# A hybrid decoder layer on one core: three edits at the boundaries of its stages

## Chip, core and metric

The kernel runs on one core of a Trainium2 chip. The metric is the device time of one execution in microseconds (us); less is better. Engines are called by their short names: PE is TensorE, DVE is VectorE, ACT is ScalarE, POOL is GpSimd, SP is SyncE.

## What is computed

One decoder layer over 2048 tokens of width 1024, all in float32. Cut to what matters here:

```python
h = rms_norm(x, pre_mix_norm)
proj = h @ w_in
y_lru = rms_norm(rg_lru(conv(proj_x)) * gelu(proj_gate), lru_out_norm)
y_ssd = rms_norm(ssd_chunked(conv(proj_xbc), dt, ...) * silu(proj_z), ssd_out_norm)
mix = concat(y_lru, y_ssd) @ w_out
x = x + rms_norm(mix, post_mix_norm)
h = rms_norm(x, pre_ffn_norm)
f = (silu(h @ w_gate) * (h @ w_up)) @ w_down
out = x + rms_norm(f, post_ffn_norm)
```

`rms_norm(x, w)` is `x * rsqrt(mean(x * x) + 1e-6) * w` over the 1024 channels of a token. The feed-forward width is 2816.

## The kernel before

**Numbers and products.** Every float32 operand of a large product is split into a rounded part and the rest (`split`, L129 to L134: a cast on ACT, a subtraction on DVE), and a product is three matmuls of 128 x 512 (`mm3`, L136 to L139). Tokens come in two blocks of 1024 (`b`), each of two halves of 512 (`j` or `hh`); a token tile has 128 tokens. The three feed-forward products are done by a seven-product scheme of 2 x 2 blocks (the operands B11, B21, T1 to T4, B22), so that sums and differences of token halves are formed first and kept in DRAM (`h_dr`, `f_dr`, `t_dr`).

**Mixer (to about 1020 us).** For each block, the columns of `w_in` stream through PE in an order written by hand; each product fills a PSUM tile named `pp`. The smaller matmuls (transposes, scans, sums) use PSUM tiles named `pq`. Both names have two buffers. Work on a finished column (`ssd_mix`, `lru_mix`) is a generator, cut by `yield`; the function `site` (L326) advances it, and calls of `site(0)` to `site(3)` stand between the products, `SITES` (L33) saying how many steps each makes. Block 0's last generator ends with `sumsq(b, 0, acc)` (L407): sixteen one-column matmuls of L118 (`rms_of`) against a vector of ones, a copy L120 and the reciprocal root `rstd_of` (L85 to L96: six small DVE operations and a root on ACT). They run at the start of block 1, behind its product for C, and the accumulator that they read is last written by L322. The result is first used in the output projection. Then come, in the program, the convolution of C, `ssd_dt3` (L443 to L459, which reads what L436 writes), `ssd_group2` (transposes L482, scores L488) and the next product.

**Output projection (about 1021 to 1363 us).** For each of 16 token tiles, in the order of `tiles` (L222), two half products go to `pp` and `pq`; L806 and L807 scale and add them; L811 to L815 do the first norm, add the input and write the row to DRAM as `x1_dr`; L816 to L818 do the second norm. The closure `turned` (L758) transposes the normed tile on PE (L761) one tile later and writes its parts to `h_dr`. The last two tiles (fourth token tile of each half of block 1) are not turned: L821 writes them normed to `hl_dr`.

**Gate and up stage (about 1363 to 2210 us).** All PSUM is eight buffers named `pf`. For each block and each of 22 steps `fi`, seven products of 12 matmuls follow each other, each into its own `pf` tile. The tiles for results are named `fo` (12 buffers, function `res`, L909): `f0`, `f1` (written by L935, L941) and, each second step, four sums (L952 to L955). Ahead of the products of steps 3 and 4 of block 0 stands `late_rows` (L855): it loads a tile from `hl_dr`, transposes it (L862), copies it to `fo` (L864) and, with the second, forms the sums L871 to L874 for `h_dr`.

**Down stage (about 2210 us to the end).** The last product, `prod_tiles(1)`, gives one token tile at a time. For each, L1089 adds it into `m1`, `square_mul` squares the row with its sum (L1025) and multiplies it in place with the norm's weight (L1026), `rstd_of` follows, and two L1048 scale it and add `x1`, each followed by a write to the output.

**What sets the order.** A scheduler orders each engine's queue when the kernel is built. Its priority is the order of the program; an instruction that is not ready by its own estimate of times is passed by a later one that is. A tile has a name, and the tiles of one name share that name's buffers.

```python
def site(n):
    if stages:
        for _ in range(SITES[n]):
            if next(stages[0], 1):
                stages.pop()
                break
```

Of the kernel before, what the change touches and what calls it, by code (L numbers as in the profile page):

```python
# [8 lines left out]
F32 = mybir.dt.float32  # L9
F32R = mybir.dt.float32r  # L10
AF = mybir.ActivationFunctionType
ALU = mybir.AluOpType
# [3 lines left out]
P = 128  # L16
T = 2048
D = 1024
KD = D // P
TB = 1024  # L20
NB = T // TB
HB = 512
# [24 lines left out]
def hybrid_layer(ctx: ExitStack, tc: tile.TileContext, x, xT, w_in, w_dt, pack, heads, rows, wa, wx, w_out, w_gu, w_dn, out):  # L47
# [13 lines left out]
    acc_dr = dram.tile([P, TB], F32, name="acc_dr")  # L61
    cs_dr = dram.tile([NB, NH, TB], F32, name="cs_dr")
    h_dr = [[dram.tile([P, 4, HB], F32, name=f"h_dr{b}_{o}") for o in range(7)] for b in range(NB)]
    hl_dr = dram.tile([2, P, D], F32, name="hl_dr")
    f_dr = [[dram.tile([P, KF, HB], F32, name=f"f_dr{b}_{o}") for o in range(7)] for b in range(NB)]
    t_dr = [dram.tile([P, KF, HB], F32, name=f"t_dr{o}") for o in range(4)]

# [2 lines left out]
    def par(n, i=0, w=None):  # L70
        o, full = PK[n]
        return pk[:, o + i:o + i + (w or 1)]
# [188 lines left out]
    with ExitStack() as fr:  # L261
# [112 lines left out]
        def lru_mix(b, i, lx, gl, acc, bdl):  # L374
            th = []
            lh, ll = (tl.tile([P, TB], F32R, name="t4", bufs=NT4) for _ in range(2))
            a.copy(out=lh, in_=lx)
            v.tensor_sub(out=ll, in0=lx, in1=lh.bitcast(F32))
            yield
            for j in range(2):  # L380
                pr = pq.tile([P, TB], F32, name="pq")
                for hh in range(2):
                    s = slice(hh * HB, (hh + 1) * HB)
                    mm3(pr[:, s], bd[:, i, j, :], bdl[i // 4][:, i % 4, j, :], lh[:, s], ll[:, s], True, True)
                t = t4()
                a.activation(out=t, in_=pr, func=AF.Tanh, scale=0.5, bias=hb[:, 8 * j + i:8 * j + i + 1])
                th.append(t)
            ci = c2[:, i:i + 1]
            av = t4()
            a.activation(out=av, in_=th[0], func=AF.Exp, scale=ci, bias=ci)  # L390
            a.activation(out=th[0], in_=th[0], func=AF.Tanh, scale=ci, bias=ci)
            a2 = t4()
            a.activation(out=a2, in_=av, func=AF.Square)
            v.scalar_tensor_tensor(out=a2, in0=a2, scalar=1.0, in1=th[0], op0=ALU.add, op1=ALU.mult)
            v.tensor_scalar(out=a2, in0=a2, scalar1=0.0, scalar2=None, op0=ALU.min)
            a.activation(out=a2, in_=a2, func=AF.Sqrt, scale=-0.25)
            v.scalar_tensor_tensor(out=th[1], in0=th[1], scalar=1.0, in1=lx, op0=ALU.add, op1=ALU.mult)
            v.tensor_mul(out=th[1], in0=th[1], in1=a2)
            v.tensor_tensor_scan(out=th[1], data0=av, data1=th[1], initial=hc[:, i:i + 1], op0=ALU.mult, op1=ALU.add)  # L399
            v.tensor_copy(out=hc[:, i:i + 1], in_=th[1][:, TB - 1:TB])  # L400
            v.tensor_mul(out=gl, in0=th[1], in1=gl)
            spill(gl, i, b)
            accum(gl, th[0], acc, i == 0)
            if i == 7:
                if b + 1 < NB:
                    yield
                    sumsq(b, 0, acc)  # L407
                else:
                    a.dma_start(out=acc_dr, in_=acc)
# [337 lines left out]
    with ExitStack() as orr:  # L747
# [36 lines left out]
        for n, t in enumerate(tiles):  # L784
            gs = gq.pop(0)
            if n == len(tiles) - 2:
                def hook(k):
                    if k % 2 == 0:
                        ops0[k // 2] = build_op(0, k // 2, hx_tile, staged)
                firsts[n] = half(gs, 0)  # L790
                firsts[n + 1] = half(gq[0], 0, hook)
                pre = load_gu(forder[0], lambda: oc.tile([P, 4, HB], F32, name="S"),
                              lambda: splp.tile([P, D], F32R, name="s_hi"), lambda: splp.tile([P, D], F32R, name="s_lo"))
            pss = [firsts.pop(n) if n in firsts else half(gs, 0), half(gs, 1)]
            if turn:
                turn.pop()()
            if n == 4:
                acc = raw_tile()
                sy.dma_start(out=acc, in_=acc_dr)
                sumsq(NB - 1, 0, acc)  # L800
            if n + 2 < len(tiles):
                gq.append(load_g(tiles[n + 2]))
            xnt = oc.tile([P, D], F32, name="xn", bufs=2)
            sy.dma_start(out=xnt, in_=x[t * P:(t + 1) * P, :])
            mx = oc.tile([P, D], F32, name="mx", bufs=2)
            a.activation(out=mx, in_=pss[0], func=AF.Copy, scale=r12[:, 0, t:t + 1])  # L806
            v.scalar_tensor_tensor(out=mx, in0=pss[1], scalar=r12[:, 1, t:t + 1], in1=mx, op0=ALU.mult, op1=ALU.add)  # L807
            junk = oc.tile([P, D], F32, name="ob")
            ss = small.tile([P, 2], F32, name="o_ss")
            rs = small.tile([P, 2], F32, name="o_rs")  # L810
            a.activation(out=junk, in_=mx, func=AF.Square, accum_out=ss[:, 0:1])  # L811
            rstd_of(ss[:, 0:1], rs[:, 0:1], 1)
            v.scalar_tensor_tensor(out=mx, in0=mx, scalar=rs[:, 0:1], in1=pmw, op0=ALU.mult, op1=ALU.mult)
            v.tensor_add(out=mx, in0=mx, in1=xnt)
            a.dma_start(out=x1_dr[t * P:(t + 1) * P, :], in_=mx)  # L815
            a.activation(out=junk, in_=mx, func=AF.Square, accum_out=ss[:, 1:2])  # L816
            rstd_of(ss[:, 1:2], rs[:, 1:2], 1)
            v.scalar_tensor_tensor(out=xnt, in0=mx, scalar=rs[:, 1:2], in1=gpf, op0=ALU.mult, op1=ALU.mult)  # L818
            b, i, j = t // NC, t % 4, (t % NC) // 4
            if b + 1 == NB and i == 3:  # L820
                a.dma_start(out=hl_dr[j], in_=xnt)  # L821
            else:
                turn.append(lambda b=b, i=i, j=j, xnt=xnt: turned(b, i, j, xnt))
    mp.close()

# [6 lines left out]
    with ExitStack() as fa:  # L832
# [21 lines left out]

        def late_rows(j, res):  # L855
            r = raw_tile()
            sy.dma_start(out=r, in_=hl_dr[j])
            xs = []
            for q in range(2):
                ps = bank()  # L860
                for k in range(4):
                    te.transpose(ps[:, k * P:(k + 1) * P], r[:, q * HB + k * P:q * HB + (k + 1) * P], ident)  # L862
                xs.append(res())
                a.copy(out=xs[-1], in_=ps)  # L864
            put = [(B11, xs[0]), (B21, xs[1])] if j == 0 else [(B22, xs[1])]
            if j == 0:
                half0.extend(xs)
            else:
                (x0, x2), (x1, x3) = half0, xs
                t1, t2, t3, t4_ = (res() for _ in range(4))  # L870
                v.tensor_sub(out=t1, in0=x1, in1=x0)  # L871
                v.tensor_sub(out=t2, in0=x3, in1=t1)
                v.tensor_sub(out=t3, in0=x3, in1=x1)
                v.tensor_sub(out=t4_, in0=x2, in1=t2)  # L874
                put += [(T1, t1), (T2, t2), (T3, t3), (T4, t4_)]
            for o, z in put:
                a.dma_start(out=h_dr[NB - 1][o][:, :, 3 * P:], in_=z.rearrange("p (k c) -> p k c", c=P))

        for b in range(NB):
# [6 lines left out]
            for fi, f in enumerate(forders[b]):  # L886
# [22 lines left out]
                def res():  # L909
                    return fo.tile([P, HB], F32, name="fo", bufs=12)  # L910
# [31 lines left out]
                k = f % KF  # L942
# [18 lines left out]
    with ExitStack() as fb:  # L961
# [57 lines left out]
                    mm3(ps, *cur[k], *(z[:, c] for z in bs[k // 2]), k == 0, k == KF - 1)  # L1019
                yield ps  # L1020

        def square_mul(y, t, e):
            junk = fy.tile([P, HB], F32, name="fjunk", bufs=1)
            ss = fy.tile([P, 1], F32, name="f_ss", bufs=4)
            a.activation(out=junk, in_=y[:, t], func=AF.Square, accum_out=ss)  # L1025
            v.tensor_mul(out=y[:, t], in0=y[:, t], in1=pfw[:, e * HB:(e + 1) * HB])  # L1026
            return ss

        def first_half(y, t, e):
# [10 lines left out]
            sy.dma_start(out=xt, in_=x1_dr[rows_of(j, t), :])  # L1040
            return xt

        def second_half(ys, t, j, e, m, xt):
            rs = fy.tile([P, 1], F32, name="f_rs", bufs=2)
            rstd_of(square_mul(ys[e], t, e), rs, 1, m)
            for z, q in ((0, a), (1, sy)):
                h = slice(z * HB, (z + 1) * HB)
                v.scalar_tensor_tensor(out=xt[:, h], in0=ys[z][:, t], scalar=rs, in1=xt[:, h],  # L1048
                                       op0=ALU.mult, op1=ALU.add)
                q.dma_start(out=out[rows_of(j, t), h], in_=xt[:, h])  # L1050

# [33 lines left out]
        for t, p in enumerate(prod_tiles(1)):  # L1085
            ms += [first_half(u2, i, 1) for i in range(len(ms), min(t + 2, NT))]
            if t + 2 < NT:
                xq.append(load_x1(0, t + 2))
            v.tensor_add(out=m1[:, t], in0=p, in1=m1[:, t])  # L1089
            second_half((m1, u2), t, 0, 0, ms[t], xq[t])  # L1090


def _cols(w, n):
# [43 lines left out]
```

## Time and profile before

| | us |
|---|---|
| median of 3 runs | 2634.25 |
| lowest, highest | 2632.26, 2636.03 |
| the profiled execution, its own time | 2635.64 |
| its span, first to last instruction | 2633.8 |
| PE busy in the span | 2613.7 (99%) |
| DVE busy | 1852.7 (70%) |
| ACT busy | 1123.6 (43%) |
| POOL busy | 1.1 (0%) |

Times in the rows below are microseconds from the span's start. A busy engine is one with an instruction in work; matmuls are pipelined, so that one of 0.39 us is followed by the next after 0.227 us. In waits, the engine named behind the arrow is the one that released the waiting one by the profile.

### The profile page before, as it was taken

The page shows a single profiled execution, that of the slowest core. Times are in us where ns is not written, and L with a number is a line of the kernel's source. Part 1 is how long each engine was busy: PE and PEld are TensorE (multiplying, and loading weights), DVE is VectorE, ACT ScalarE, POOL GpSimd, SP SyncE. Part 2 cuts the span into 40 slices and gives each one's busy share as a digit, 9 for nine tenths or more (in the row PEclk, how much of TensorE's full clock was granted, in tenths as well). Part 3 has the DMA queues.
Part 4 walks back from the last instruction along what each step waited for, and adds up shares of the span by engine and source line. Part 5 has one row for each costly group of instructions (what it writes and reads, how often), then busy time and mean ns, then how long its engine had stood idle before and what let it go on. Part 6 is the DMA issues. An engine that isn't in the chain of part 4 may idle for free.

```text
span 2633.8 us, 31866 instructions
## 1 busy us (share of the span) xinstructions
PE 2613.7 (99%) x12360; PEld 2170.4 (82%) x12360; DVE 1852.7 (70%) x2716; ACT 1123.6 (43%) x1340; POOL 1.1 (0%) x8
## 2 busy tenths in 40 slices
PE   9999999999999999999999999999999999999998
PEld 7888888888888887888877888888888888888887
DVE  7997878888777767544478777678767675334676
ACT  6544456754535777332253222234222222322443
POOL 0000000000000000000000000000000000000000
PEclk9999999999999999999999999999999999999999
DMA  5342461223334635543454333235333325444664
GB/s 211 111 131 73 128 201 65 82 88 113 95 96 150 210 96 205 154 136 123 143 196 150 134 104 116 81 121 195 104 100 110 106 92 173 151 139 153 212 245 140
DMA packets 189975, 357.79 MB, mean 136 GB/s; under 512 B 18528, under 2 KB 91616, under 8 KB 189824
## 3 DMA queue, kind: packets, MB, share of 16 engines
q1 hardware_dynamic: 88912, 256.56, 30.3%
q10 hardware_dynamic: 100912, 99.20, 10.8%
q8 instruction: 97, 1.59, 0.2%
q14 instruction: 54, 0.44, 0.1%
HBM read 253.86 MB, written 101.84 MB: 135 GB/s over the span
## 4 chain that ended last, share of the span: by engine, by line
PE 93%; DVE 3%; ACT 2%; DMA 1%; issue 1%; DVEq 0%; ACTq 0%; SPq 0%
PE pf L139 16%; PE pf L138 16%; PE pf L137 16%; PE pp L137 11%; PE pp L139 10%; PE pp L138 10%; PE pq L137 3%; PE pq L138 3%; PE pq L139 3%; PE pq L530 1%; PE pq L542 1%; PE pq L551 1%; DMA t_dr<-L 1%; PE pq L514 1%; DVE t L399 0%
## 5 line engine op out<-in xcount | busy, mean ns | idle before, releaser
L137 PE MATMUL pp<-hx,s_hi 128*128 128x512 f32 x1392 | 548.2, 394 | 1.2 <-ACT hx L243 0.7
L139 PE MATMUL pp<-hx,s_lo 128*128 128x512 f32 x1392 | 545.4, 392 | 0.5 <-DVE s_lo L133 0.5
L138 PE MATMUL pp<-hx,s_hi 128*128 128x512 f32 x1392 | 543.6, 391 | 0.6 <-DVE hx L244 0.6
L132 ACT CAST s_hi<-raw 128x1024 fp32r<-128x1024 f32 (+1 forms) x167 | 170.3, 1022 | 380.2 <-PE pp L138 123.0
L139 PEld LDWEIGHTS pp<-hx,s_lo 128*128 128x128 f32 x1392 | 261.7, 188 | 56.5 <-issue 0.9
L137 PEld LDWEIGHTS pp<-hx,s_hi 128*128 128x128 f32 x1392 | 261.8, 188 | 56.2 <-issue 1.6
L138 PEld LDWEIGHTS pp<-hx,s_hi 128*128 128x128 f32 x1392 | 261.9, 188 | 54.2 <-DVE hx L244 1.0
L139 PE MATMUL pf<-hx,s_lo 128*128 128x512 f32 x704 | 273.9, 389 | 0.7 <-DVE s_lo L133 0.7
L137 PE MATMUL pf<-hx,s_hi 128*128 128x512 f32 x704 | 274.2, 389 | 0.4 <-ACT s_hi L132 0.4
L138 PE MATMUL pf<-hx,s_hi 128*128 128x512 f32 x704 | 273.9, 389 | 0.0
L133 DVE TENSOR_TENSOR s_lo<-raw,s_hi 128x1024 fp32r<-128x1024 f32 (+1 forms) x167 | 198.0, 1187 | 64.1 <-ACT s_hi L132 55.7
L978 DVE TENSOR_TENSOR d_lo<-draw,d_hi 128x1024 fp32r<-128x1024 f32 (+1 forms) x110 | 121.5, 1129 | 171.4 <-ACT d_hi L977 170.1
L132 ACT CAST s_hi<-S 128x1024 fp32r<-128x1024 f32 x86 | 90.3, 1050 | 268.6 <-PE pf L138 247.3
L138 PE MATMUL pf<-d_lo,d_hi 128*128 128x512 f32 x504 | 196.1, 389 | 0.0
L977 ACT CAST d_hi<-draw 128x1024 fp32r<-128x1024 f32 (+1 forms) x110 | 104.9, 980 | 213.5 <-PE pf L138 181.6
L139 PE MATMUL pf<-d_hi,d_lo 128*128 128x512 f32 x504 | 195.9, 389 | 0.0
L137 PE MATMUL pf<-d_hi 128*128 128x512 f32 x504 | 194.6, 389 | 0.0
L139 PEld LDWEIGHTS pf<-hx,s_lo 128*128 128x128 f32 x704 | 132.1, 188 | 28.9 <-DVE s_lo L133 1.6
L137 PEld LDWEIGHTS pf<-hx,s_hi 128*128 128x128 f32 x704 | 132.1, 188 | 28.2 <-ACT s_hi L132 0.9
L138 PEld LDWEIGHTS pf<-hx,s_hi 128*128 128x128 f32 x704 | 132.1, 188 | 27.4
L302 DVE SCALAR_TENSOR_TENSOR lx<-xr,pk,lx 128x1024 f32<-128x1024 f32 x108 | 138.2, 1279 | 10.4 <-ACT lx L299 9.3
L138 PE MATMUL pf<-hy,s_hi 128*128 128x512 f32 x356 | 138.8, 390 | 1.5 <-DVE hy L718 1.4
(339 smaller groups left out, 4518.2 us busy)
## 6 DMA issues: line engine op xcount, KB each, us to landing
raw<-w_gu_dram SPq DMA_DIRECT2D x86, 512.0 KB, 4.2
f_dr<-fo ACTq DMA_DIRECT2D x154, 256.0 KB, 4.5
raw<-w_in_dram SPq DMA_DIRECT2D x72, 512.0 KB, 3.4
draw<-f_dr SPq DMA_DIRECT2D x57, 512.0 KB, 4.3
L<-cs_dr SPq DMA_DIRECT2D x32, 512.0 KB, 5.3
g_dr<-t ACTq DMA_DIRECT2D x32, 512.0 KB, 3.4
raw<-g_dr SPq DMA_DIRECT2D x32, 512.0 KB, 5.0
raw<-h_dr SPq DMA_DIRECT2D x26, 512.0 KB, 4.4
```

The source lines that it names most:

```text
L132: a.copy(out=hi, in_=raw)
L133: v.tensor_sub(out=lo, in0=raw, in1=hi.bitcast(F32))
L137: te.matmul(o, lhsT=wh, rhs=hi, start=start, stop=False)
L138: te.matmul(o, lhsT=wh, rhs=lo, start=False, stop=False)
L139: te.matmul(o, lhsT=wl, rhs=hi, start=False, stop=stop)
L302: v.scalar_tensor_tensor(out=y, in0=xr[:, k:k + TB], scalar=cw(k), in1=y, op0=ALU.mult, op1=ALU.add)
L514: te.transpose(pt[:, c].rearrange("p j d -> p (j d)"), xc[:, c * P:(c + 1) * P], ident)
L530: te.matmul(pst[:, c, :], lhsT=Bt[:, c, :], rhs=xe[:, c].rearrange("p j d -> p (j d)"), start=True, stop=True)
L542: te.matmul(po[:, c, :], lhsT=(sc[:, xi, :] if c == 0 else U[:, c - 1, :]), rhs=C[:, c * P:(c + 1) * P], start=True, stop=True)
L551: te.matmul(py[64 * j:64 * j + 64, c, :], lhsT=xd[:, c, j, :], rhs=L[:, j, c, :], start=True, stop=True)
L977: a.copy(out=hi, in_=r)
L978: v.tensor_sub(out=lo, in0=r, in1=hi.bitcast(F32))
```

## The change

1. In `lru_mix`, one more `yield` stands before `sumsq(b, 0, acc)` of block 0. With the calls of `site` as they are, it is then reached by `site(0)` of the first `ssd_proj` of block 1 and not by `site(3)` of its first `ssd_group`.
2. The second norm of the last two tiles leaves the output projection. `late_rows` loads the row from `x1_dr`, squares it in two halves on ACT (with two more `fo` tiles as scratch), does `rstd_of`, scales the row with `tensor_scalar` on DVE, transposes it, and applies the norm's weight in eight copies of 128 columns. `hl_dr` is gone.
3. In the last product, L1026 writes into the PSUM tile of the product (`room`) and not over `m1`, and the first L1048 reads it there.

```diff
--- before.py
+++ after.py
@@ -61,7 +61,6 @@
     acc_dr = dram.tile([P, TB], F32, name="acc_dr")
     cs_dr = dram.tile([NB, NH, TB], F32, name="cs_dr")
     h_dr = [[dram.tile([P, 4, HB], F32, name=f"h_dr{b}_{o}") for o in range(7)] for b in range(NB)]
-    hl_dr = dram.tile([2, P, D], F32, name="hl_dr")
     f_dr = [[dram.tile([P, KF, HB], F32, name=f"f_dr{b}_{o}") for o in range(7)] for b in range(NB)]
     t_dr = [dram.tile([P, KF, HB], F32, name=f"t_dr{o}") for o in range(4)]
 
@@ -403,6 +402,7 @@
             accum(gl, th[0], acc, i == 0)
             if i == 7:
                 if b + 1 < NB:
+                    yield
                     yield
                     sumsq(b, 0, acc)
                 else:
@@ -813,13 +813,11 @@
             v.scalar_tensor_tensor(out=mx, in0=mx, scalar=rs[:, 0:1], in1=pmw, op0=ALU.mult, op1=ALU.mult)
             v.tensor_add(out=mx, in0=mx, in1=xnt)
             a.dma_start(out=x1_dr[t * P:(t + 1) * P, :], in_=mx)
-            a.activation(out=junk, in_=mx, func=AF.Square, accum_out=ss[:, 1:2])
-            rstd_of(ss[:, 1:2], rs[:, 1:2], 1)
-            v.scalar_tensor_tensor(out=xnt, in0=mx, scalar=rs[:, 1:2], in1=gpf, op0=ALU.mult, op1=ALU.mult)
             b, i, j = t // NC, t % 4, (t % NC) // 4
-            if b + 1 == NB and i == 3:
-                a.dma_start(out=hl_dr[j], in_=xnt)
-            else:
+            if b + 1 < NB or i < 3:
+                a.activation(out=junk, in_=mx, func=AF.Square, accum_out=ss[:, 1:2])
+                rstd_of(ss[:, 1:2], rs[:, 1:2], 1)
+                v.scalar_tensor_tensor(out=xnt, in0=mx, scalar=rs[:, 1:2], in1=gpf, op0=ALU.mult, op1=ALU.mult)
                 turn.append(lambda b=b, i=i, j=j, xnt=xnt: turned(b, i, j, xnt))
     mp.close()
 
@@ -854,14 +852,24 @@
 
         def late_rows(j, res):
             r = raw_tile()
-            sy.dma_start(out=r, in_=hl_dr[j])
+            t0 = (NB - 1) * TB + j * HB + 3 * P
+            sy.dma_start(out=r, in_=x1_dr[t0:t0 + P, :])
+            ss = small.tile([P, 2], F32, name="o_ss")
+            rs = small.tile([P, 2], F32, name="o_rs")
+            for q in range(2):
+                a.activation(out=res(), in_=r[:, q * HB:(q + 1) * HB], func=AF.Square, accum_out=ss[:, q:q + 1])
+            v.tensor_add(out=ss[:, 0:1], in0=ss[:, 0:1], in1=ss[:, 1:2])
+            rstd_of(ss[:, 0:1], rs[:, 0:1], 1)
+            v.tensor_scalar(out=r, in0=r, scalar1=rs[:, 0:1], scalar2=None, op0=ALU.mult)
             xs = []
             for q in range(2):
                 ps = bank()
                 for k in range(4):
                     te.transpose(ps[:, k * P:(k + 1) * P], r[:, q * HB + k * P:q * HB + (k + 1) * P], ident)
                 xs.append(res())
-                a.copy(out=xs[-1], in_=ps)
+                for k in range(4):
+                    c = slice(k * P, (k + 1) * P)
+                    a.activation(out=xs[-1][:, c], in_=ps[:, c], func=AF.Copy, scale=par("g_ffn", 4 * q + k))
             put = [(B11, xs[0]), (B21, xs[1])] if j == 0 else [(B22, xs[1])]
             if j == 0:
                 half0.extend(xs)
@@ -1019,11 +1027,11 @@
                     mm3(ps, *cur[k], *(z[:, c] for z in bs[k // 2]), k == 0, k == KF - 1)
                 yield ps
 
-        def square_mul(y, t, e):
+        def square_mul(y, t, e, room=None):
             junk = fy.tile([P, HB], F32, name="fjunk", bufs=1)
             ss = fy.tile([P, 1], F32, name="f_ss", bufs=4)
             a.activation(out=junk, in_=y[:, t], func=AF.Square, accum_out=ss)
-            v.tensor_mul(out=y[:, t], in0=y[:, t], in1=pfw[:, e * HB:(e + 1) * HB])
+            v.tensor_mul(out=y[:, t] if room is None else room, in0=y[:, t], in1=pfw[:, e * HB:(e + 1) * HB])
             return ss
 
         def first_half(y, t, e):
@@ -1040,12 +1048,13 @@
             sy.dma_start(out=xt, in_=x1_dr[rows_of(j, t), :])
             return xt
 
-        def second_half(ys, t, j, e, m, xt):
+        def second_half(ys, t, j, e, m, xt, room=None):
             rs = fy.tile([P, 1], F32, name="f_rs", bufs=2)
-            rstd_of(square_mul(ys[e], t, e), rs, 1, m)
+            rstd_of(square_mul(ys[e], t, e, room), rs, 1, m)
             for z, q in ((0, a), (1, sy)):
                 h = slice(z * HB, (z + 1) * HB)
-                v.scalar_tensor_tensor(out=xt[:, h], in0=ys[z][:, t], scalar=rs, in1=xt[:, h],
+                y = room if z == e and room is not None else ys[z][:, t]
+                v.scalar_tensor_tensor(out=xt[:, h], in0=y, scalar=rs, in1=xt[:, h],
                                        op0=ALU.mult, op1=ALU.add)
                 q.dma_start(out=out[rows_of(j, t), h], in_=xt[:, h])
 
@@ -1087,7 +1096,7 @@
             if t + 2 < NT:
                 xq.append(load_x1(0, t + 2))
             v.tensor_add(out=m1[:, t], in0=p, in1=m1[:, t])
-            second_half((m1, u2), t, 0, 0, ms[t], xq[t])
+            second_half((m1, u2), t, 0, 0, ms[t], xq[t], p)
 
 
 def _cols(w, n):
```

## Rows read from the trace of the kernel before

**Rows 1.** The page, chain that ended last: shares of the span by engine.
```profile
PE 93%; DVE 3%; ACT 2%; DMA 1%; issue 1%; DVEq 0%; ACTq 0%; SPq 0%
```

**Rows 2.** PE's waits: total us, times, longest us.
```profile
PE pq L118 <- DVE acc L322: 1.0, 1, 1.0
```

**Rows 3.** Timeline, PE and DVE around L118: start, us, engine, instruction, idle before.
```profile
546.15 0.39 PE L139 MATMUL pp<-hx,s_lo 128*128 128x512 f32 x1
...
547.51 1.95 PE L118 MATMUL pq<-ones,acc 128*128 128x1 f32 x16 [0.97 <-DVE acc L322]
...
550.79 0.60 PE L137 MATMUL pp<-hx,s_hi 128*128 128x512 f32 x1
...
554.44 0.39 PE L137 MATMUL pp<-hx,s_hi 128*128 128x512 f32 x1
...
554.53 0.28 DVE L436 TENSOR_TENSOR dtx<-dt,amat 128x128 f32<-128x128 f32 x1
...
557.42 0.38 PE L443 MATMUL pq<-dtx,tri 128*128 128x128 f32 x2
...
829.34 1.84 PE L118 MATMUL pq<-ones,acc 128*128 128x1 f32 x16
```

**Rows 4.** Windows: us, busy of PE, PEld, DVE, ACT, POOL; clock; DMA, GB/s.
```profile
552.00:554.00 2.00, 2.00 (x6) 1.57 (x5) 1.83 (x10) 1.72 (x2) 0.00 (x0) 0.50 0.72 262
```

**Rows 5.** Windows, same columns, entry of the gate stage.
```profile
1379.00:1386.00 7.00, 5.28 (x20) 3.10 (x19) 6.19 (x14) 4.96 (x7) 0.00 (x0) 1.00 0.58 219
1386.00:1393.00 7.00, 6.03 (x25) 4.35 (x24) 6.54 (x10) 3.99 (x6) 0.00 (x0) 1.00 0.47 169
1393.00:1424.00 31.00, 31.00 (x138) 25.67 (x137) 27.32 (x40) 10.12 (x13) 0.00 (x0) 1.00 0.42 141
```

**Rows 6.** Timeline of ACT, the last tile's second norm.
```profile
1378.69 1.28 ACT L91 ACT_TABLE_LOAD   x1
1379.98 0.20 ACT L91 ACTIVATE rs_s<-rs_v 128x1 f32<-128x1 f32 x1
```

**Rows 7.** Groups by line, DVE, 1362 to 1393: count, busy us, mean ns.
```profile
L818 DVE SCALAR_TENSOR_TENSOR xn<-mx,o_rs,gpf 128x1024 f32<-128x1024 f32 x2 | 2.6, 1282 | 0.0
```

**Rows 8.** Timeline of the tail, ACT and DVE.
```profile
2626.60 0.63 ACT L1025 ACTIVATE fjunk<-m 128x512 f32<-128x512 f32 x1 [5.67 <-DVE m L1089]
...
2627.35 0.69 DVE L1026 TENSOR_TENSOR m<-m,pfw 128x512 f32<-128x512 f32 x1 [0.85 <-ACT fjunk L1025]
2627.96 0.21 DVE L90 TENSOR_SCALAR rs_v<-f_ss,f_ms 128x1 f32<-128x1 f32 x1
...
2629.41 0.75 DVE L1048 SCALAR_TENSOR_TENSOR fx<-m,f_rs,fx 128x512 f32<-128x512 f32 x1
```

**Rows 9.** Timeline, DVE and PE, start of the output projection.
```profile
1044.65 1.28 DVE L807 SCALAR_TENSOR_TENSOR mx<-pq,r,mx 128x1024 f32<-128x1024 f32 x1
...
1056.66 0.39 PE L138 MATMUL pp<-hx,s_hi 128*128 128x512 f32 x1
...
1058.71 1.04 PE L761 MATMUL pq<-ident,xn 128*128 128x128 f32 x8
1059.50 0.48 PE L137 MATMUL pq<-wob,s_hi 128*128 128x512 f32 x1
```

**Rows 10.** Timeline, PE, ACT and DVE, steps 3 and 4 of the gate stage.
```profile
1424.32 1.03 PE L862 MATMUL pf<-ident,raw 128*128 128x128 f32 x8
...
1425.98 1.05 ACT L864 COPY fo<-pf 128x512 f32<-128x512 f32 x2
...
1444.25 1.03 PE L862 MATMUL pf<-ident,raw 128*128 128x128 f32 x8
...
1450.07 0.68 DVE L955 TENSOR_TENSOR fo<-fo 128x512 f32<-128x512 f32 x1
...
1451.76 1.08 ACT L864 COPY fo<-pf 128x512 f32<-128x512 f32 x2 [3.11 <-DVE ft L920]
```

**Rows 11.** Line L395, DVE: count, ns min/median/max, first and last start.
```profile
L395 DVE TENSOR_SCALAR t<-t x16: 684/693/695, 350.9 to 1019.1; 128x1024 f32<-128x1024 f32 x16
```

## The prediction

> **What bounds the kernel now.** I read the chain of waits first, to see which engine's work is the span. TensorE (PE) holds 93% of it [rows 1]: one missing microsecond of PE's is one of the kernel's, and VectorE (DVE) and ScalarE (ACT) count only where PE waits for them, or behind PE's last matmul. So the second view is PE's own waits. The reader is to see that one of them lies exactly at an edit: 1.0 us before the sum of squares L118, for the accumulator [rows 2]. The third is the timeline there. The matmul before starts at 546.15, steps are 0.227, so L118 was due at 546.38 and came at 547.51: 1.13 late. Shortly after, nine steps take from 550.79 to 554.44, 3.65 us instead of 2.04 [rows 3], and the granted clock reads 0.50, the 1.2 GHz level [rows 4]. The sum at 829.34 had nothing to wait for and no such stretch behind it [rows 3]. Fourth come windows at the entry of the gate stage: PE runs 138 matmuls in 31 us when undisturbed (0.225 each), but 20 and 25 in two stretches of 7 us [rows 5], where 31 fit. Last is the tail, 8 us in which PE is done [rows 8].
>
> **Part 1, the sum of squares.** The extra yield puts L118 behind the dt sums (L443 to L447) and the B transposes and scores (L482, L488) in program order. Gain: 1.13 of wait and 3.65 − 2.04 = 1.61 of half clock, 2.74. Its 16 matmuls and the small DVE operations stay. Its new PSUM buffer is the one of the B transposes, which ACT must copy out; I take 0.1 for that. Bounds: gain 2.7 (no wait) to 0 (a wait as long as the old one, with its clock). Next late: L443 started at 557.42, its input from L436 was written at 554.81 [rows 3]; PE comes 2.7 earlier, at 554.7, when DVE has also lost a wait for L118. That cover is just used up, hence at most 0.1. **Gain 2.6.**
>
> **Part 2, what leaves the gate entry.** For each of two tiles DVE loses L818 (1.28, [rows 7]) and seven one-column operations of up to 0.21 (L90 [rows 8]); ACT loses a square over 1024 columns, a root and, with the last tile, a table load of 1.28 [rows 6] and the load back. The two writes of hl_dr leave ACT's queue; the loads on SP stay, with x1_dr as source, which is written earlier. POOL has nothing. PE misses 11.2 + 6.2 matmuls in the two stretches [rows 5], 17.4 × 0.225 = 3.9 us. DVE is busy 6.19 and 6.54 of 7 there, so DVE is what PE waits for, and 2 × 1.28 + 14 × 0.2 = about 5 us are taken off it. I take 3.4, as the last weight splits also hang on loads; bounds 1.5 to 3.9. **Gain 3.4.**
>
> **Part 2, what enters the gate stage.** By busy time it is cheap: ACT and DVE have room. What counts is where the chain can begin, and two orders bind it.
>
> First, PSUM: buffers of one name are handed out in program order, and a tile takes its own when its first writer is placed. In the projection the transposes of tile 0 (L761) precede, in the program, the second half of the third tile's product; both use pq. L807 at 1044.65 ended reading the second pq buffer at 1045.93, so both were free. Still PE did not begin that half. It went on with a first half in pp that comes later still in the program (the row at 1056.66 is one of its matmuls), did L761 at 1058.71, and only then took up pq again [rows 9]. The later tile was ready and stood behind the earlier one that wasn't.
>
> Second, the SBUF name fo shows the same. The second tile's transposes ended at 1445.28, and ACT sat idle for 3.11 us, but the copy L864 into fo came at 1451.76, behind L955 at 1450.07 [rows 10], which first writes the last earlier fo tile.
>
> Now the edit. The squares write their scratch into fo (res()), so they can't start before the place of L864: 1425.98 and 1451.76 [rows 10]. The transposes need the squares, and their two PSUM banks (pf) are asked for ahead of those of the block's seven products. All PE work of this stage goes through pf, so PE stands until the chain is done. Before, it went through in time because the row came normalised. The chain: two squares, 0.63 + 0.75 (one square till its reader [rows 8]); a table load 1.28; from the root to the end of the correction 1.24 (L90 at 2627.96 to L1048 at 2629.41 is 1.45 [rows 8], less 0.21 for L90 itself); tensor_scalar 0.69 [rows 11]. Together 4.59. The first: 1425.98 + 4.59 = 1430.57, PE has been free since 1424.32 [rows 10]: 6.2 us. The second: 1451.76 + 4.59 = 1456.35 against 1444.25: 12.1 us. Each stall is longer than the 1.13 after which the clock fell, so I add 1.6 for each [rows 3]: 3.2. Bounds: 5 + 8.5 and no clock price (if DVE writes the sums earlier) is 13.5; 6.8 + 12.8 and twice the clock price is 26. **Loss 21.5.**
>
> After the transposes eight copies of 128 columns replace two of 512, and ACT loads the table back; PE is in the next products by then and 8 banks cover it. Cover gone, it would be once the load's 1.28 [rows 6] and the copies' surplus. DVE's other work has no one waiting.
>
> The chain holds one table load per tile, and the trace shows the load at 1378.69 and the root right behind it at 1379.98 [rows 6]. The Trainium skill, "ScalarE: Activation LUTs", section "What ACT_TABLE_LOAD costs", gives a load of 1.28 us and a drain of 1.38 us on top for each change of set. By it each stall would be 1.4 us longer and the kernel near 2652 us, an estimate from that page. The row has the same load and no drain, so the sum goes without and the page's reading gets no chance of its own; it stays inside the range.
>
> **Part 3, the tail.** The weight product L1026 started 0.75 after the square, for it overwrote what the square reads; L90 came 0.61 behind its start [rows 8]. With PSUM as target it runs beside the square, and L90 follows the square. The last L1048 reads PSUM; L807 does so in 1.28, as long as L818 without PSUM [rows 7, 9]. **Gain 0.6**, bounds 0 to 0.7. Tiles before the last are covered by PE.
>
> **Sum.** + 21.5 − 2.6 − 3.4 − 0.6 = + 14.9. The profiled execution took 2635.64, 1.84 more than its span, and would become 2650.5; it lay 1.39 above the median, and from the median of 2634.25 the sum gives **2649.2**. Its own range: 13.5 − 2.7 − 3.9 − 0.7 = + 6.2 and 26 − 0 − 1.5 − 0 = + 24.5, of which I keep 2640 to 2656, as the ends need all bounds at once.
>
> **Rivals.** *No stall* (faster): one of the two orders doesn't bind, the squares run early in idle time of ACT or the products pass the transposes. Place: 1424 to 1457. For it: ACT sat idle there for 3.11 us [rows 10], and both orders are read from one instance each. Against: rows 9 and 10 agree. It gives − 6.6, 2627.6. It decides once the squares of both tiles run before the block ahead has ended its products. *One stall*: L864 came late at 1451.76 for another reason, say the writes that ACT issues ahead of it, so that the second chain runs early and only the first stall stays: 6.2 + 1.6 − 6.6 = + 1.2, 2635.5, within the noise. For it: the profile names another releaser for that idle time than L955 [rows 10]. Against: an instruction that is ready is passed by none of lower priority. *The sum stays where it is*: PE's place for L118 is set by when the accumulator is thought ready, not by the yield, and the 2.6 don't come: 2651.8. For it: the matmuls around L118 are all of pp [rows 3], so it stands inside a product now and not between two. Against: its PSUM name pq is handed out in program order [rows 9], so L488 goes ahead.
>
> **Numbers.** Forecast 0.65, sum stays 0.10 (both slower), one stall 0.07, no stall 0.18. About 0.2%, 5.3 us, is what a measurement of this kernel can tell from no change. So slower 0.75, same 0.07, faster 0.18. Range: 2640 to 2656 alone would leave out more than 2 in 10, so it reaches down to the case without a stall: 2627 to 2656.
>
> **What would show it.** Right: a PE wait of 6 us before the first L862 place and one of about 12 us before the second, each with a granted clock of 0.5 behind; squares of 512 columns behind L941 and L955; no wait before L118 and no half clock near 551; more than 28 matmuls in each stretch of 7 us at the entry; L90 straight behind the last square. Wrong: PE full between 1415 and 1460, or squares there early; then the time is below 2630. A wait before L118 in its new place would show part 1 wrong.

## The result and the profile after

| | before | after |
|---|---|---|
| median, us (6 runs each) | 2634.56 | 2653.49 |
| lowest to highest | 2631.39 to 2636.03 | 2651.81 to 2655.78 |
| span of the profiled execution | 2633.8 | 2654.0 |
| mean granted clock of PE | 0.999 | 0.995 |

The ratio is 1.0074, with a 95% interval of 1.0061 to 1.0087: the change costs 16 to 23 us. 2649.2 was predicted, with 2627 to 2656 as the range, and slower at 0.75.

The profile's chain of work that ended last, by engine, answers to [rows 1]: PE has lost two points of the span.

```profile
PE 91%; DVE 4%; ACT 3%; DMA 1%; issue 1%; ACTq 0%; DVEq 0%; SPq 0%
```

PE's waits (total us, times, longest) answer to [rows 2]. The wait for the accumulator is gone. Three others of 1.5 us or more are new, and the first of them is the result:

```profile
PE pf L868 <- DVE raw L863: 18.7, 2, 12.5
PE pq L136 <- ACT wob L242: 1.9, 1, 1.9
PE pq L443 <- DVE dtx L436: 1.5, 1, 1.5
```

**The first stall.** The timeline of PE, ACT and DVE at step 3 of the gate stage (start, us, engine, instruction, idle before):

```profile
1420.63 0.39 PE L138 MATMUL pf<-hy,s_lo 128*128 128x512 f32 x1
...
1421.97 0.63 ACT L948 ACTIVATE ft<-ft 128x512 f32<-128x512 f32 x1
...
1422.50 0.61 ACT L860 ACTIVATE fo<-raw 128x512 f32<-128x512 f32 x1
...
1423.84 1.28 ACT L90 ACT_TABLE_LOAD   x1
1424.02 0.69 DVE L949 TENSOR_TENSOR fo<-ft 128x512 f32<-128x512 f32 x1
...
1425.13 0.20 ACT L90 ACTIVATE rs_s<-rs_v 128x1 f32<-128x1 f32 x1
...
1427.15 1.11 PE L868 MATMUL pf<-ident,raw 128*128 128x128 f32 x4 [6.13 <-DVE raw L863]
```

The squares L860 begin only behind the last instruction of step 2 on ACT, 1.9 us after PE's last matmul of that step. Then the chain runs as a whole, and PE stands from 1420.86, when its next step was due, to 1427.15: 6.29 us.

**The second stall.** The same view one step later:

```profile
1449.02 0.39 PE L138 MATMUL pf<-hy,s_lo 128*128 128x512 f32 x1
...
1453.86 3.29 ACTq L965 DMA_DIRECT2D f_dr<-fo  x4
...
1455.07 0.68 DVE L963 TENSOR_TENSOR fo<-fo 128x512 f32<-128x512 f32 x1
1457.20 0.63 ACT L860 ACTIVATE fo<-raw 128x512 f32<-128x512 f32 x1 [6.21 <-issue]
...
1461.95 0.66 PE L868 MATMUL pf<-ident,raw 128*128 128x128 f32 x2 [12.54 <-DVE raw L863]
```

Here the squares stand behind the four sums of step 3 (the last is L963) and the four writes L965 that ACT issues for them. PE was due at 1449.25 and comes at 1461.95: 12.70 us.

The windows (us, busy of PE, PEld, DVE, ACT, POOL with counts; clock; DMA share, GB/s) show what follows each stall, and the entry of the stage, which answers to [rows 5]:

```profile
1379.00:1386.00 7.00, 7.00 (x33) 5.79 (x32) 7.00 (x13) 2.47 (x4) 0.00 (x0) 1.00 0.76 255
1386.00:1393.00 7.00, 7.00 (x33) 5.79 (x32) 7.00 (x10) 3.64 (x5) 0.00 (x0) 1.00 0.45 152
...
1427.00:1432.00 5.00, 4.85 (x17) 4.19 (x18) 0.09 (x1) 2.18 (x8) 0.00 (x0) 0.54 0.47 146
...
1462.00:1466.00 4.00, 4.00 (x14) 3.52 (x15) 1.41 (x3) 2.18 (x8) 0.00 (x0) 0.54 0.24 82
```

The entry is full, 33 and 33 matmuls for 20 and 25. Behind both stalls the granted clock reads 0.54, nearly all of it at the 1.2 GHz level, the lower of the two.

### The profile page after: what moved, and what is told of

Read it like the earlier page. It is cut to its first block, busy times and chain, and to the rows that moved or that the text cites. A ratio compares the mean times of both kernels' runs of the same rounds, so it can differ in the third digit from the quotient of the medians.

```text
span 2654.0 us, 31884 instructions
## 1 busy us (share of the span) xinstructions
PE 2615.9 (99%) x12360; PEld 2174.2 (82%) x12360; DVE 1854.3 (70%) x2718; ACT 1129.7 (43%) x1359; POOL 1.1 (0%) x8
## 4 chain that ended last, share of the span: by engine, by line
PE 91%; DVE 4%; ACT 3%; DMA 1%; issue 1%; ACTq 0%; DVEq 0%; SPq 0%
PE pf L138 16%; PE pf L136 16%; PE pf L137 16%; PE pp L136 10%; PE pp L138 10%; PE pp L137 10%; PE pq L136 3%; PE pq L138 3%; PE pq L137 3%; PE pq L530 1%; PE pq L551 1%; PE pq L542 1%; DVE lx L301 1%; PE pq L514 1%; DMA raw<-g_dr 0%
```

## The experiments

Seven kernels were run. The medians stand against the kernel before, run on the same chip.

### 1. The norm moved, the other two parts undone

```diff
-                    yield
                     yield
                     sumsq(b, 0, acc)
...
-            second_half((m1, u2), t, 0, 0, ms[t], xq[t], p)
+            second_half((m1, u2), t, 0, 0, ms[t], xq[t])
```

> The second norm of the two late tiles is moved as in the change; the extra yield and the PSUM target are undone. Theory (the move alone makes the loss): both stalls of PE ahead of the transposes are there as after the change, 6.3 and 12.7 us beyond the usual step, each with about 2.0 us of half clock behind it, together 23.0; the entry of the gate stage is full, a gain of about 4. So about 19 us over the kernel before. If the new wait of 2.0 us near 1037 us (and the 1.6 us of half clock behind it) comes from the extra yield, it is gone here. Rival (the edits act on each other): one of the stalls is shorter by 2 us or more, or the wait near 1037 us is still there.

Measured: 2650.91 against 2634.33, ratio 1.0064 (1.0049 to 1.0079), so 16.6 us. PE's waits:

```profile
PE pf L867 <- DVE raw L862: 18.6, 2, 12.4
...
PE pq L117 <- DVE acc L321: 1.0, 1, 1.0
```

Part 2 alone makes the loss, and both stalls are the same to 0.1 us. The half clock cost less than expected, 1.40 and 1.45 us by the way from the transposes to the next mark, which is 1.2 of the 2.4 us by which the total is under the expectation. The wait near 1037 us isn't there.

One thing doesn't add up. By their rows (experiments 5 and 6, and the half clock) the other two parts should make the changed kernel 0.7 us faster than this one. Its median is 2.6 us higher, and all its runs (2651.81 to 2655.78) lie above all of these (2649.61 to 2651.47). The last section comes back to this.

### 2. The scratch of the squares in a buffer of another name

```diff
+            junk = raw_tile()
             for q in range(2):
-                a.activation(out=res(), in_=r[:, q * HB:(q + 1) * HB], func=AF.Square, accum_out=ss[:, q:q + 1])
+                h = slice(q * HB, (q + 1) * HB)
+                a.activation(out=junk[:, h], in_=r[:, h], func=AF.Square, accum_out=ss[:, q:q + 1])
```

> The change whole, but the squares of both late tiles write their scratch into a tile named raw and not into two tiles named fo. Nothing else differs. Theory (the order of the fo buffers holds the squares back): the squares of both tiles run while the products of the step ahead are still going, no wait of PE is left ahead of the transposes, and with them 19.0 us of stalls and 4.0 us of half clock go: 23 us under the changed kernel, some 3 us under the kernel before. Rival A (ACT is busy, or the row comes late, so that the chain starts where it did): both stalls stay and the time is that of the changed kernel within 2 us. Rival B (the transposes wait for something else, such as a PSUM bank): the squares run early and PE stands all the same.

Measured: 2629.74 against 2634.33, ratio 0.9981 (0.9971 to 0.999). That is 24 us under the changed kernel, and faster than the kernel before too. ACT's timeline, the first tile:

```profile
1395.41 0.63 ACT L862 ACTIVATE raw<-raw 128x512 f32<-128x512 f32 x1 [1.68 <-DMA raw<-x_dr]
```

The square now waits for nothing but its row, and runs 21 us ahead of the transposes at 1416.85; the second tile's last square runs at 1426.35, 10 us ahead of the transposes at 1436.79. PE is full in the windows that held the stalls:

```profile
1420.00:1427.00 7.00, 7.00 (x32) 5.82 (x31) 3.58 (x5) 6.40 (x17) 0.00 (x0) 1.00 0.71 225
1449.00:1462.00 13.00, 13.00 (x59) 10.77 (x58) 11.11 (x16) 4.80 (x6) 0.00 (x0) 1.00 0.32 98
```

ACT's load, the late row and the eight copies are the same as in the changed kernel. Only the scratch differs (one tile named `raw` for two named `fo`), so the order of the `fo` buffers held the squares back, and rivals A and B fall.

### 3. Only the second tile's scratch apart

```diff
+            junk = raw_tile() if j else None
             for q in range(2):
-                a.activation(out=res(), in_=r[:, q * HB:(q + 1) * HB], func=AF.Square, accum_out=ss[:, q:q + 1])
+                h = slice(q * HB, (q + 1) * HB)
+                a.activation(out=res() if j == 0 else junk[:, h], in_=r[:, h], func=AF.Square, accum_out=ss[:, q:q + 1])
```

> As the changed kernel, but only the second late tile has its scratch in a tile named raw; the first keeps its two tiles named fo. Theory (each stall is set by its own tile's scratch): the first stall stays, about 6.3 us and up to 0.6 us more, since a square of the second tile may run between; the second, 12.7 us and its 2.0 us of half clock, goes. So about 14 us under the changed kernel and 5 to 6 us over the kernel before. Rival (the second stall follows from the first, or from the four writes that ACT issues ahead of its squares): the second stall is 10 us or more still.

Measured: 2637.26 against 2634.33, ratio 1.0013 (1.0003 to 1.0022): 2.9 us over the kernel before, where 5 to 6 were expected. By its rows, the stall is 6.90 and the half clock behind it 2.69, less 4.44 for the entry, 1.17 for the yield and 0.61 for the tail (all measured below): 3.4. The expectation had left the yield and the tail out. PE's waits hold one stall, and ACT's timeline shows the second tile's first square right behind the last of the first tile:

```profile
PE pf L870 <- DVE raw L865: 6.7, 1, 6.7
```

```profile
1419.13 0.61 ACT L862 ACTIVATE fo<-raw 128x512 f32<-128x512 f32 x1
...
1419.74 0.61 ACT L862 ACTIVATE raw<-raw 128x512 f32<-128x512 f32 x1
```

The second tile's transposes follow their step without a gap, at 1446.39 behind a matmul at 1446.17. So the four writes are no cause of their own: in the changed kernel they stood ahead of the squares because the squares' scratch stood behind the sums.

### 4. The transposes behind the products of their step

```diff
             v.tensor_scalar(out=r, in0=r, scalar1=rs[:, 0:1], scalar2=None, op0=ALU.mult)
+            return r
+
+        def late_turn(j, res, r):
             xs = []
...
-                    late_rows(fi - 3, res)
+                    lr = late_rows(fi - 3, res)
...
+                if b + 1 < NB and 3 <= fi < 5:
+                    late_turn(fi - 3, res, lr)
```

> As the changed kernel, scratch in fo as there, but the transposes, their copies and sums of each late tile stand behind the seven products of their step in the program and not ahead of them; load, squares, correction and scaling stay where they were. Theory (PE stands because the transposes' PSUM tiles come ahead of the products' in program order): the chain of squares may start as late as it did, but PE has the step's 84 matmuls, 19 us, to do meanwhile, and no wait is left: 23 us under the changed kernel, some 3 us under the kernel before, as with the scratch apart. Rival (it is the lateness of the chain itself that costs): a stall of 6 us or more is left ahead of the transposes in their new place.

Measured: 2629.73 against 2634.33, ratio 0.9985 (0.9975 to 0.9994). The squares are no earlier than in the changed kernel: the second tile's first runs 11.0 us after PE's last matmul of step 3 (8.2 there), and stands in ACT's timeline behind the writes of the sums and the first tile's copies.

```profile
1443.01 3.31 ACTq L968 DMA_DIRECT2D f_dr<-fo  x4
...
1449.14 0.63 ACT L860 ACTIVATE fo<-raw 128x512 f32<-128x512 f32 x1 [0.60 <-ACT fo L875]
```

And PE hardly waits for the chain, as its waits show:

```profile
PE pf L871 <- DVE raw L863: 0.4, 1, 0.4
```

So both orders are needed for the loss: squares that can't begin early (`fo`) and transposes that can't be passed (`pf`). Taking away either one takes away all of it.

### 5. The yield alone

```diff
                 if b + 1 < NB:
                     yield
+                    yield
                     sumsq(b, 0, acc)
```

> The kernel before with the extra yield alone. Theory: the wait of 1.13 us before the sum of squares and the 1.61 us of half clock behind it go, but PE now comes to L443 earlier not by these 2.7 us alone but also by the sum's own 1.9 us, and waits there 1.7 us for dtx, with no half clock behind it. Net about 1.1 us under the kernel before. Rival A (the prediction's sum): no more than 0.1 us of wait at L443, net 2.6 us. Rival B (the edits act on each other): the wait at L443 came from the other edits and is gone here. The wait near 1037 us that the changed kernel's profile has is not expected: it was absent from two of the three kernels run so far with the yield in them.

Measured: 2633.57 against 2634.28, ratio 0.9997 (0.9988 to 1.0005), too small to tell from no change. The rows tell more. In DVE's and PE's timeline before L444 (L443 in the kernel before):

```profile
551.25 0.39 PE L138 MATMUL pp<-hx,s_hi 128*128 128x512 f32 x1
551.41 0.29 DVE L113 TENSOR_TENSOR dt<-sp,sp 128x128 f32<-128x128 f32 x1
551.62 1.28 DVE L302 SCALAR_TENSOR_TENSOR lx<-xr,pk,lx 128x1024 f32<-128x1024 f32 x1
552.81 0.28 DVE L437 TENSOR_TENSOR dtx<-dt,amat 128x128 f32<-128x128 f32 x1
...
553.15 0.49 PE L444 MATMUL pq<-dtx,tri 128*128 128x128 f32 x2 [1.51 <-DVE dtx L437]
```

The kernel of experiment 6 has no yield and is at the same time before (a matmul that both traces have starts at 507.64 here and at 507.58 there). In it the same stretch goes so:

```profile
551.95 0.29 DVE L113 TENSOR_TENSOR dt<-sp,sp 128x128 f32<-128x128 f32 x1
552.30 0.28 DVE L436 TENSOR_TENSOR dtx<-dt,amat 128x128 f32<-128x128 f32 x1
552.64 1.28 DVE L302 SCALAR_TENSOR_TENSOR lx<-xr,pk,lx 128x1024 f32<-128x1024 f32 x1
...
555.15 0.38 PE L443 MATMUL pq<-dtx,tri 128*128 128x128 f32 x2
```

With the yield PE is due at 551.48, 3.67 us earlier, while `dtx` comes 0.51 later, since DVE's order was built anew and a convolution step of 1.28 us now stands ahead of it. The next PE mark that both have, a matmul before a wait near 999 us, tells the net gain:

```profile
997.92 0.39 PE L137 MATMUL pp<-hx,s_hi 128*128 128x512 f32 x1
```

```profile
999.03 0.39 PE L137 MATMUL pp<-hx,s_hi 128*128 128x512 f32 x1
```

The first is the yield's kernel, the second experiment 6: 997.92 − 507.64 = 490.28 against 999.03 − 507.58 = 491.45. Up to there the yield is worth 1.17 us, as the theory had it; rivals A and B fall. The other profiles agree: the same two matmuls are 490.3 us apart in experiments 2, 3 and 4, which have the yield, and 491.4 to 491.9 in the kernel before and experiments 1 and 7, which don't. In the changed kernel's profile it is 490.9. The wait near 1037 us is absent here.

### 6. The PSUM target alone

```diff
-            second_half((m1, u2), t, 0, 0, ms[t], xq[t])
+            second_half((m1, u2), t, 0, 0, ms[t], xq[t], p)
```

> The kernel before with the weight product of the last norm written to PSUM, alone. Theory: the product runs beside the square, the correction starts 0.6 us earlier behind it, and the end comes 0.6 us earlier; no difference anywhere else. That is under what the timed runs can tell, so the rows of the tail decide: from the start of the last addition into m1 to the first row of the correction, 2.15 us before, 1.54 us here. Rival (the operations on PSUM are longer): the product or the last scaling takes 0.1 us or more over 0.70 and 0.75 us, and part of the 0.6 is given back.

Measured: 2633.22 against 2634.28, ratio 0.9992 (0.9984 to 1.0). The tail's first addition in the kernel before, then the tail in this kernel's timeline, which answers to [rows 8]:

```profile
2625.81 0.69 DVE L1089 TENSOR_TENSOR m<-pf,m 128x512 f32<-128x512 f32 x1 [2.47 <-PE pf L139]
```

```profile
2624.55 0.69 DVE L1090 TENSOR_TENSOR m<-pf,m 128x512 f32<-128x512 f32 x1 [3.07 <-PE pf L139]
2625.28 0.70 DVE L1026 TENSOR_TENSOR pf<-m,pfw 128x512 f32<-128x512 f32 x1
2625.34 0.63 ACT L1025 ACTIVATE fjunk<-m 128x512 f32<-128x512 f32 x1 [6.27 <-DVE m L1090]
2626.09 0.21 DVE L90 TENSOR_SCALAR rs_v<-f_ss,f_ms 128x1 f32<-128x1 f32 x1
...
2627.54 0.75 DVE L1049 SCALAR_TENSOR_TENSOR fx<-pf,f_rs,fx 128x512 f32<-128x512 f32 x1
```

From the addition to L90 are 1.54 us, against 2.15 in the kernel before, and the operations on PSUM are no longer than those without (0.70 for 0.69, 0.75 for 0.75). The 0.6 is there, up to the last scaling. What lies behind it varies by more: from the end of the last scaling to the end of the span are 3.0 us here and in the kernel before, but 4.3 in the changed kernel's profile. Why was not tried.

### 7. The scratch apart, without the yield

The edit of experiment 2, with one `yield` taken out again as in experiment 1.

> The scratch apart as in the second experiment, with the extra yield undone. Theory: no stall in the gate stage, its entry full (about 4 us), the tail 0.6 us shorter, and the wait of 1.13 us before the sum of squares back with its 1.61 us of half clock, while the wait at L443 is gone: about 4.6 us under the kernel before and 1.1 us over the second experiment's kernel. Rival (the yield is worth the 2.6 us of the prediction): 2.6 us over it.

Measured: 2629.37 against 2634.28, ratio 0.998 (0.9971 to 0.9988), 4.9 us faster. The yield's 1.17 us can't be seen between this kernel and that of experiment 2 (2629.37, and 2629.74 with the yield), so whether the end of the kernel keeps that gain isn't shown. The trace of this kernel is a clean measure for the gate stage, as it has neither stall nor the old norms. Its PE rows: first matmul of the stage, last before the first transposes, those transposes, last before the second, those, and the last of the kernel.

```profile
1361.52 0.39 PE L136 MATMUL pf<-hx,s_hi 128*128 128x512 f32 x1
...
1418.42 0.39 PE L138 MATMUL pf<-hy,s_lo 128*128 128x512 f32 x1
1418.65 0.38 PE L869 MATMUL pf<-ident,raw 128*128 128x128 f32 x2
...
1438.35 0.39 PE L138 MATMUL pf<-hy,s_lo 128*128 128x512 f32 x1
1438.58 0.38 PE L869 MATMUL pf<-ident,raw 128*128 128x128 f32 x2
...
2619.72 0.39 PE L138 MATMUL pf<-d_hi,s_lo 128*128 128x512 f32 x1
```

Entry: 1418.42 − 1361.52 = 56.90 us here. In experiment 5, where the norms are in their old place, the same two rows are 1420.42 − 1359.08 = 61.34. The entry's gain is 4.44 us.

Half clock: from the first transposes to the next step's end are 1438.35 − 1418.65 = 19.70 us here and 1449.02 − 1427.15 = 21.87 in the changed kernel, 2.17 more. From the second transposes to PE's last matmul are 1181.14 here and 2644.89 − 1461.95 = 1182.94 there (its last matmul is at 2644.89), 1.80 more.

## Why the prediction was right, point by point

| step of the prediction, us | predicted | measured |
|---|---|---|
| two stalls at the transposes | + 6.2 + 12.1 | + 6.29 + 12.70 |
| half clock behind them | + 3.2 | + 2.17 + 1.80 |
| entry of the gate stage | − 3.4 | − 4.44 |
| the sum of squares | − 2.6 | − 1.17 |
| the tail | − 0.6 | − 0.61 |
| sum | + 14.9 | + 16.7 |

The stalls and the half clock are those of the changed kernel; the other parts are taken from experiments 5, 6 and 7, where each stands undisturbed. The medians differ by 18.9 and the interval is 16 to 23, so the measured parts lie inside it, but 2.2 us of the middle have no part of their own. That the forecast's sum came within 2 us of the measured parts is partly luck: the sum of squares was 1.4 too hopeful and the entry 1.0 too cautious, and these two nearly cancel.

The profiled spans differ by 20.2. Of the other 3.5 us there, 3.7 are the wait at 1037 us and its half clock, below, 1.2 lie behind the last scaling, and the way to the output projection was 1.5 shorter than the yield explains.

**The mechanism was right.** The two orders were read from one instance each [rows 9, 10], and experiments 2 and 4 release one each: either takes the whole loss away. The rivals *no stall* and *one stall* are out for the changed kernel, but each is real as a kernel: experiment 3 is the one stall, and its 2.9 us over the kernel before is near the 1.2 that the rival gave. *The sum stays where it is* is out too: L118 of the kernel before runs at 562.12 in the changed kernel, behind the dt sums.

**The stalls.** The chain was put at 4.59 us and took 4.65 (1422.50 to 1427.15) and 4.75. The starts of the squares were put by the place of the copy, 1.66 and 7.51 us after PE was due at its transposes [rows 10]; they came 1.64 and 7.95 after. At the second, ACT was issuing the four writes until 1457.15, straight ahead of the square. One sign of the prediction didn't come at the first: "squares of 512 columns behind L941". L941 is L949 in the changed kernel and starts at 1424.02, when both squares had run. They stood behind L948, the last instruction of step 2 on ACT, as the copy did before. So the name `fo` set the squares' place in ACT's queue there; they did not wait until the earlier `fo` tile was written.

**No drain.** The load at 1423.84 took 1.28 us, and the root follows at 1425.13, as [rows 6] had it. The Trainium skill, "ScalarE: Activation LUTs", section "What ACT_TABLE_LOAD costs", adds a drain of 1.38 us for a change of set. The trace does not agree: with it the root would have come at 1426.5. That the result lies near the 2652 of that reading is chance; its surplus is in other terms.

**The half clock** was priced at 1.6 each by one instance [rows 3]. Five instances are there now: 2.17 and 1.80 (the changed kernel), 1.40 and 1.45 (experiment 1), 2.69 (experiment 3), 1.9 in the mean. The term was 0.8 too low. The windows show why the price varies: the level fell within each of these stalls, and only what was left of the low stretch when PE came back cost time. Behind the first stall PE worked at 0.50 from 1427.15 to 1431.40, 4.25 us, and from 1431.50 on the clock reads 0.99; half of 4.25 is 2.1. In experiment 3 it was low until past 1429.20, 5.4 us after the transposes at 1423.78, and half of that is 2.7. A longer stall was not a dearer one: 12.70 us were followed by 1.80, 6.90 by 2.69.

**The entry** was mis-sized: PE's missing matmuls were counted in two windows of 7 us, 3.9 us in all, and 3.4 taken with 3.9 as the upper bound. The whole entry lost 4.44, outside the bound, and all of it lies in those two windows: the matmul at 1392.57 in the kernel before is already 4.44 later, from the stage's first matmul, than the same one in experiment 7. What was wrong is the count. A window counts each matmul that runs in it, also one that began before it, so that a full one of 7 us shows 33, as above, and not the 31 that "fit" by the steps. The loads that were held against the term show as no wait of PE there.

**The sum of squares** is the step that failed. The prediction said of L443: "PE comes 2.7 earlier, at 554.7, ... hence at most 0.1". Three things were missing. The sum's own time, 1.8 us from L118 to the next matmul, also moved behind L443; four matmuls of the next product came ahead of it in exchange (0.9). PE was thus due 3.67 earlier, not 2.74. And DVE's order changed, with `dtx` 0.51 later. With 0.93 and 0.51 on top of the 0.1 that the prediction allowed, the wait is 1.5, which is what the profile names. The wait's end is set by L436, as named; its size was not.

**The tail** came as predicted, in the rows. The PSUM target costs DVE nothing that a row shows.

## What to carry to other kernels

A scratch tile is an operand like any other: if its name is shared with results that come late, the instruction that writes it is late too, however early its data are. Ask of each instruction that is put ahead of a block what its buffers stand behind, and of each that waits what stands behind it in the buffers of its output. When a piece of work is moved behind a deadline, the next deadline comes nearer by the wait that goes and by the work itself; and the order of the other engines is built anew. And where a window's count of instructions is used, compare it with the count of a full window, not with the window's length divided by the step.

## What the runs showed of the hardware

**The clock after a wait.** The longer wait was not the one that brought the clock down. Before L118 PE stood 1.13 us, then did sixteen one-column matmuls, and the clock fell to 0.50 [rows 3, 4]. Before L443 it stood 1.67 us in experiment 5, then did twenty matmuls of 128 columns, and the window behind it reads 1.00. So does the one around the sum in its new place at 561.17, where the same sixteen matmuls come without a wait.

```profile
553.00:556.00 3.00, 2.85 (x22) 2.30 (x23) 2.94 (x5) 2.05 (x5) 0.00 (x0) 1.00 0.00 0
561.00:566.00 5.00, 5.00 (x32) 4.36 (x31) 1.21 (x7) 0.57 (x3) 0.00 (x0) 1.00 0.98 305
```

What makes the difference was not tried and stays open. For a forecast it means that 1.6 us of half clock can't be put behind a wait by its length alone.

**A wait that comes and goes.** In the profile of the changed kernel PE waits 1.86 us at the start of the output projection, and the clock falls behind it. The cast that it needs stands on ACT behind another that waited for a load (PE and ACT timelines, and a window):

```profile
1038.71 0.52 PE L136 MATMUL pq<-wob,s_hi 128*128 128x512 f32 x1 [1.86 <-ACT wob L242]
```

```profile
1036.99 1.04 ACT L131 CAST s_hi<-raw 128x1024 fp32r<-128x1024 f32 x1 [2.92 <-DMA raw<-g_dr]
1037.94 0.72 ACT L242 ACTIVATE wob<-raw,pk 128x512 fp32r<-128x512 f32 x1
```

```profile
1040.00:1042.00 2.00, 2.00 (x6) 1.53 (x5) 0.75 (x1) 1.31 (x2) 0.00 (x0) 0.50 0.83 246
```

Of the other profiles only that of experiment 4 has it, with 1.0 us; experiments 2, 3 and 5, with the same yield, don't. So the yield doesn't always bring it. But none of the four profiles without the yield has it, so that the yield makes it likelier isn't excluded. It isn't simply that PE comes early: experiment 1, without the yield, begins the projection at 1017.35, the changed kernel at 1018.32, and experiment 1 doesn't wait. Why the load is late in some executions was not tried. From the projection's first matmul to the gate stage's first are 345.4 us in this profile and 341.7 in that of experiment 5: the wait and its half clock cost 3.7. If most executions of the changed kernel have it, it would account for the some 3 us that don't add up in experiment 1. The timed runs have no rows, so that stays open. An edit's price is better taken between two rows of one trace than from two spans.
